# Up projections of a four-layer trunk: one matmul over 512 latent columns in place of two over 256

## The chip, the cores and the metric

The kernel runs on one core of a Trainium2 chip. The metric is device microseconds of one execution, as the median of three runs. The profile is one further execution, recorded by the hardware profiler; times in it are microseconds from the start of its span, unless marked ns.

## What is computed

A trunk of four layers over 512 latent tokens and 256 context tokens with 1024 channels, in fp32. Each layer normalises, modulates by vectors made from a conditioning vector, mixes tokens (short gated convolution in layers 0 and 3, windowed attention in layer 1, differential attention in layer 2), and then runs a ConvGLU with 2816 inner channels. Cut to what matters:

```python
def conv_ffn(x, w_up, conv_w, conv_b, w_down):
    a, g = jnp.split(x @ w_up, 2, axis=-1)
    g = dwconv(g, conv_w) + conv_b
    return (jax.nn.silu(g) * a) @ w_down

def short_conv_mixer(x, w_in, w_conv, w_out):
    b_gate, c_gate, h = jnp.split(x @ w_in, 3, axis=-1)
    return (b_gate * dwconv(c_gate * h, w_conv)) @ w_out

for i in range(DEPTH):
    xn = modulate(rmsnorm(h, g1), sh1, sc1)
    ...
    h = h + gt1 * y
    h = h + gt2 * conv_ffn(modulate(rmsnorm(h, g2), sh2, sc2), *ffns[i])
    if ctx_after:
        hc = hc + cg1 * yc
        hc = hc + cg2 * conv_ffn(modulate(rmsnorm(hc, g2), ch2, cc2), *ffns[i])
```

The context stream takes part up to the mixer of layer 2; from layer 2's ConvGLU on there are latents alone.

## The kernel before

Activations lie with channels on the 128 partitions and tokens along the columns: 8 chunks of channels, `hL` with 512 latent columns and `hC` with 256 context columns each. The streams are cut into parts of 256 columns: `CTXS` (the context), `H0` and `H1` (the halves of the latents); `LAT` stands for all 512. `parts_of` turns regions (`CTXS`, `LAT`) into parts.

**Precision.** Every operand of a large product is kept as two numbers, a rounded one and the rest (`wh` and `wl` of a weight, `xh` and `xl` of an activation), and `mm3` (L160 to L162) issues three matmuls for each product: `wh` by `xh`, `wh` by `xl`, `wl` by `xh`. The first operand is the stationary one, 128x128, and each matmul has a weight load of its own (engine PEld).

**Phases.** There are eight: a mixer and a ConvGLU in each layer. At the end of one, `boundary` weaves the last down products, part by part, with the norm of the next phase (`norm_steps`): squares, statistics, then for each chunk a modulated value (`nt`, L376), its rounded part by ScalarE (`xh`, L377) and the rest by VectorE (`xl`, L382). Each part has tiles of its own for `xh` and `xl`, 256 columns wide, 8 chunks each. They lie in a pool that is opened anew for each phase on the side `self.xside`, with the other tiles of a mixer or ConvGLU (`gp`, `cv`, `mh`, `ml`) on the opposite side. The side is left at first (L1127), and each attention mixer turns it over when it ends (L875 for layer 1, L1102 for layer 2).

**Up projections.** `project` computes one output chunk of 128 channels: for each part, 8 chunks of input channels by three matmuls into a PSUM tile `ps` (two of them, 1024 columns each: latents in columns 0 to 511, context behind them), or into `pb` for some. The first few projections of a phase are begun by `phase_start` for all parts but the last and finished later, when the last part's norm is there; they are named `pre` in the trace, both pieces of them. The others go through `projected` at once and carry the names `pg` and `pa` (ConvGLU) and `pc`, `ph`, `pb` (convolution). `phase_start` takes two projections where both streams run and four where the latents run alone.

**Units.** A ConvGLU has 22 units: `pg` is copied to `gp` (L575), the convolution's taps run on VectorE (L508 to L510), silu on ScalarE, and the product with `pa` is split into `mh` and `ml`. A convolution mixer has 8, of `pc`, `ph` and `pb`. Units go up two at a time and come down through `down_steps`: products `pd`, latents over 512 columns in one matmul, context over 256, added to `hL` and `hC` by VectorE (L430). The attention mixers project tokens instead (`tok_project`, L670 to L672, name `pj`): there the x tile, 128 tokens of it, is the stationary operand and 512 columns of weights move.

**Side work.** The modulation vectors of later phases are computed in between by VectorE (L289) and summed over partitions by GpSimd (`partition_all_reduce`, L291), once for each stream that needs the vector (`ada_vecs`, L237).

**Order.** Every engine's instructions are put in order when the kernel is built, by a scheduler that places waits where tiles are written and read; only a few DMAs and splits are pinned to the order of the program.

Of the kernel before, what the change touches and what calls it, by code (L numbers as in the profile page):

```python
# [10 lines left out]
F32R = mybir.dt.float32r  # L11
# [34 lines left out]
class Trunk:  # L46
# [1 line left out]
        self.tc, self.nc, self.A, self.out, self.stop = tc, tc.nc, A, out, stop  # L48
        self.xside = "left"

    # ---------------------------------------------------------------- weights
    def plan_weights(self):
        A = self.A
        w = []
# [55 lines left out]
        return hi, lo  # L110

    def prefetch(self, n):
        """Splits the next n weights, one a step, and lifts the limit."""
        for _ in range(n):
            if len(self.wready) < self.wpos + 5:
                self._split(True)
            self.wlimit = max(self.wlimit, len(self.wready))
            yield
# [10 lines left out]
        self.wready[i] = None  # L129
        return r  # L130

    # ---------------------------------------------------------------- helpers
    def ps(self, name):
        return self.pp.tile([P, 1024], F32, name=name, tag="ps", bufs=2)

# [40 lines left out]
            self.nc.tensor.matmul(ps[:, t * P:(t + 1) * P], r[:, t:t + 1].to_broadcast([P, P]), self.ident,  # L176
                                  start=True, stop=True)

    # ---------------------------------------------------------------- setup
    def setup(self, es):  # L180
        tc, nc, A = self.tc, self.nc, self.A
        self.cp = cp = es.enter_context(tc.tile_pool(name="const", bufs=1))
# [49 lines left out]
        for k in range(KC):  # L232
            self.tc.keep_in_program_order(self.nc.sync.dma_start(self.h[0][k], self.A["x"][k]))

    # ---------------------------------------------------------------- ada
    def ada_vecs(self, l, m):
        return (0, 1) if l < 2 or (l == 2 and m < 2) else (0,)  # L237

    def ada_first(self):
        """Shift and scale of the first norms: a chunk of channels at a time, straight on the tensor engine."""  # L240
        nc = self.nc
        for j in range(KC):
            if j in EARLY:
                self._fetch(True)
                self._split()
            acc = self.pb(f"adaf{j}")
            for i in range(2):
                raw = self.first.tile([P, KC // 2, 2 * P], F32, name=f"adaf{j}_{i}", tag="raw", bufs=5)
                self.tc.keep_in_program_order(nc.sync.dma_start(raw, self.A["l0_ada_first"][j, i]))
                for k in range(KC // 2):  # L250
                    nc.tensor.matmul(acc[:, :2 * P], self.cwide[:, i * KC // 2 + k], raw[:, k],
                                     start=i + k == 0, stop=i * k == KC // 2 - 1)
            row = self.ntmp("adarow")[:, :2 * P]
            nc.scalar.copy(row, acc[:, :2 * P])
            for m in range(2):
                nc.tensor.transpose(acc[:, (2 + m) * P:(3 + m) * P], row[:, m * P:(m + 1) * P], self.ident)
            cols = acc[:, 2 * P:].rearrange("p (m v e) -> p m v e", m=2, v=2)[:, :, :, 0]
            md = self.cp.tile([P, 2, 2], F32, name=f"md{j}", tag="md", bufs=KC)
            nc.vector.tensor_tensor(md, cols, self.ada_b[0][:, 0:2, j:j + 1].to_broadcast([P, 2, 2]), ALU.add)
            gs = self.cp.tile([P, 2], F32, name=f"gs{j}", tag="gs", bufs=KC)  # L260
            nc.vector.scalar_tensor_tensor(gs, md[:, 1, :], 1.0, self.g1[0][:, j:j + 1].to_broadcast([P, 2]),
                                           ALU.add, ALU.mult)
            self.mods1.append((md[:, 0, :], gs))
            yield
# [41 lines left out]
            if next(self.ada, "end") == "end":  # L306
                break

    # ---------------------------------------------------------------- norm
    def norm_steps(self, l, s, second, first):  # L310
        """RMS norm and modulation of one stream: a step for the square of each chunk, then the rest.
        The first norms scale the chunks by the statistics before the modulation is there."""
        nc = self.nc
        sid, T, off = s
        xp = self.xp
# [37 lines left out]
        yield  # L353
        rb = pst[:, T:2 * T]
        self.bcast_cols(rb, r, nt)
        xs, ts = [], []
        self.xn_next[s] = xs
        for k in range(KC):
            hi = xp.tile([P, T], F32R, name=f"xh{sid}_{off}_{k}", tag=f"xh{sid}", bufs=KC * (2 - sid))
            lo = xp.tile([P, T], F32R, name=f"xl{sid}_{off}_{k}", tag=f"xl{sid}", bufs=KC * (2 - sid))  # L360
            xs.append((hi, lo))
            if first:
                t = self.first.tile([P, T], F32, name=f"nt{sid}_{off}_{k}", tag="nt", bufs=3 * KC)
                nc.vector.tensor_tensor(t, h[k], rb, ALU.mult)
                ts.append(t)
# [17 lines left out]
            if k % 2 or first:  # L383
                yield

    # ---------------------------------------------------------------- pair structure
    def project(self, src, xn, parts, name, acc=None, split=False):
        """Projects some parts of the streams; acc is what an earlier call for other parts returned."""
        if acc is None:
            if split:  # L390
                out = {sid: self.pb(name) for sid, _, _ in parts}
            else:
                ps = self.ps(name)
                out = {0: ps[:, :SEQ], 1: ps[:, SEQ:TOK], "all": ps}
            acc = self.get_w(src), out
        (wh, wl), out = acc
        for s in parts:
            sid, T, off = s
            o = out[sid][:, off:off + T]
            for k in range(KC):  # L400
                xh, xl = xn[s][k]
                w = slice(k * P, (k + 1) * P)
                self.mm3(o, wh[:, w], wl[:, w], xh, xl, k == 0, k == KC - 1)
        return acc

    def phase_start(self, srcs, xn, regions):
        """The first projections of a phase leave the last part of the streams to the end."""
        n = PRM["nb"] if len(regions) == 2 else PRM["nl"]
        self.pre = [self.project(src, xn, parts_of(regions)[:-1], f"pre{i}", split=i >= 2) for i, src in enumerate(srcs[:n])]

    def projected(self, src, xn, regions, name):
        parts = parts_of(regions)
        if self.pre:
            return self.project(src, xn, parts[-1:], name, self.pre.pop(0))[1]
        return self.project(src, xn, parts, name)[1]

    def down_steps(self, units, ws, gate, parts, pools):
        nc = self.nc
# [12 lines left out]
                    yield  # L431

    def begin(self, s, first=False):
        """The norm of stream s for the phase that follows, if it takes part there."""
        if self.next is None or s not in parts_of(self.next[1]):
            return iter(())
        if self.xn_next is None:
            self.close_x()
            self.open_x()
            self.xn_next = {}  # L440
        return self.norm_steps(self.next[0], s, self.next[2], first)

    def boundary(self, seq, gate, before=()):
        """The last down products, stream by stream, woven with the norms of the next phase."""
        prev = list(before)
        for s, units, ws, last in seq:
            nrm = self.begin(s) if last else iter(())
            for _ in self.down_steps(units, ws, gate, [[s]], (self.pt, self.pb)):
                next(nrm, None)
                for g in prev:  # L450
                    next(g, None)
            if last:
                for g in prev:
                    for _ in g:
                        pass
                prev = []
            prev.append(nrm)
        for g in prev:
            for _ in g:
                pass  # L460

    def timeline(self, tasks, rate):
        """Interleaves generators: each task (begin, end, steps, generator) takes its steps evenly over its slots,
        and the filler takes rate steps a slot."""
        live = []
        tasks = sorted(tasks, key=lambda t: t[0])
        at, due, end = 0, 0.0, max(t[1] for t in tasks)
# [61 lines left out]

    @staticmethod  # L530
    def pair_order(n):
        """Units go up and down in groups, each going down while the next goes up; the last four go down together."""
        order = []
        for g in range(0, n - 2, GRP):
            order += [("up", c) for c in range(g, g + GRP)]
            if g:
                order += [("down", c) for c in range(g - GRP, g)]
        return order + [("up", n - 2), ("up", n - 1)] + [("down", c) for c in range(n - 4, n)]
# [66 lines left out]
        gate = {sid: self.mods[l, sid][:, 2, :] for sid, _, _ in streams}  # L605
        self.pairs(KC, up, A[f"l{l}_sc_out"], gate, streams, ticks)

    # ---------------------------------------------------------------- attention pieces
    def rope_table(self, l, which, yt):
        """Gain, and cosine and sine with the gain in them, of one of q and k."""  # L610
        nc, A = self.nc, self.A
        g = yt.tile([P, 2, HD], F32, name=f"gain{l}{which}")
        nc.sync.dma_start(g, A[f"l{l}_gain"][:, "qk".index(which)])
# [58 lines left out]
                mm(o, xh, wl[:, w], start=False, stop=k == KC - 1)  # L672
            post(tt, o)

    # ---------------------------------------------------------------- layer 1 mixer
    def window_gqa(self, xn):
        nc, A = self.nc, self.A
        yc = self.tc.tile_pool(name="y1", bufs=1, side=self.yside)
# [203 lines left out]
        self.boundary([(H1, final[H1], ws[1], True)], gate, [nrm, nrm0])  # L882
        mc.__exit__(None, None, None)

    # ---------------------------------------------------------------- layer 2 mixer
    def diff_attn(self, xn):
        nc, A = self.nc, self.A
        yc = self.tc.tile_pool(name="y2", bufs=1, side=self.yside)
# [214 lines left out]
        self.boundary([(s, *self.last, True) for s in (H0, H1)], gate)  # L1103
        mc.__exit__(None, None, None)

    # ---------------------------------------------------------------- whole
    def run(self):
        tc, nc = self.tc, self.nc
        es = ExitStack()
# [183 lines left out]
```

## Time and profile before

| what | value |
|---|---|
| median of the runs | 3337.18 us |
| runs | 3334.94, 3337.18, 3341.43 us |
| span of the profiled execution | 3339.3 us |
| what the profile shows around the span | nothing |
| mean granted TensorE clock | 0.972 of 2.4 GHz |
| matmuls | 22364 |

The profiled execution has no time of its own beside its span; the span lies 2.1 us above the median of the runs and within their range. Engines are PE (TensorE's matmuls), PEld (its weight loads), DVE (VectorE), ACT (ScalarE), POOL (GpSimd) and SP (SyncE). Matmuls overlap in the pipeline, and their ends are modelled, so their durations add up to more than the time that they take.

### The profile page before, as it was taken

The numbers are of one execution on the slowest core, as the hardware profiler recorded it, in microseconds if no ns is written. First come the engines' busy times: TensorE is split into PE (matmuls) and PEld (weight loads), VectorE is DVE, ScalarE is ACT, GpSimd is POOL, SyncE is SP. The second block draws the span as 40 slices with busy tenths as digits, with TensorE's granted clock in tenths as the row PEclk, the third lists the DMA queues.
The fourth block names the chain that finished last, engine by engine and source line by source line (L and its number), as shares of the span: only waits on it lengthen the run. The fifth ranks groups of instructions, "written<-read, shape, count | busy, mean of one in ns | idle before, by whom it ended". The sixth has DMA issues, their size and how long they took to land.

```text
span 3339.3 us, 53917 instructions
## 1 busy us (share of the span) xinstructions
PE 3272.2 (98%) x22364; PEld 2979.7 (89%) x22364; DVE 2207.4 (66%) x3278; ACT 1127.0 (34%) x1888; POOL 686.3 (21%) x578
## 2 busy tenths in 40 slices
PE   8999999999998999999999999999999999999999
PEld 7999999989986778999999987677899999999999
DVE  5775887786565676676666576366687765565555
ACT  4113322222333565422222243356432323242222
POOL 2132223211132333111000134255211110010000
PEclk9999999999996899899999999899999999999999
DMA  6431443442110000333333112401265532222322
GB/s 226 139 108 52 152 132 110 134 132 77 52 65 19 14 21 6 102 108 113 110 127 112 60 54 79 142 29 54 68 202 161 179 112 89 95 89 84 101 89 76
DMA packets 105237, 323.29 MB, mean 97 GB/s; under 512 B 12576, under 2 KB 27552, under 8 KB 104992
## 3 DMA queue, kind: packets, MB, share of 16 engines
q1 hardware_dynamic: 100512, 313.26, 29.0%
q0 software_dynamic: 4480, 6.58, 0.9%
q8 instruction: 176, 2.88, 0.3%
q14 instruction: 69, 0.57, 0.1%
HBM read 311.26 MB, written 8.53 MB: 96 GB/s over the span
## 4 chain that ended last, share of the span: by engine, by line
PE 93%; DVE 4%; ACT 1%; DMA 1%; issue 1%; POOL 0%; SPq 0%; ACTq 0%; DVEq 0%; POOLq 0%
PE pd L160 8%; PE pd L161 8%; PE pd L162 8%; PE pa L161 6%; PE pa L160 6%; PE pa L162 6%; PE pg L160 6%; PE pg L162 6%; PE pg L161 6%; PE pj L670 3%; PE pj L671 3%; PE pj L672 3%; PE psS L980 2%; PE pO L826 2%; PE pPT L816 1%; PE psS L979 1%
## 5 line engine op out<-in xcount | busy, mean ns | idle before, releaser
L108 ACT CAST wh<-wr 128x1024 fp32r<-128x1024 f32 x380 | 392.2, 1049 | 1282.1 <-issue 524.9
L109 DVE TENSOR_TENSOR wl<-wr,wh 128x1024 fp32r<-128x1024 f32 x380 | 497.9, 1323 | 233.0 <-ACT wh L108 231.6
L160 PE MATMUL pd<-mh,wh 128*128 128x256 f32 (+1 forms) x1712 | 568.6, 333 | 9.9 <-DVE hC L430 9.2
L161 PE MATMUL pd<-ml,wh 128*128 128x256 f32 (+1 forms) x1712 | 564.1, 330 | 0.3 <-DVE ml L1057 0.3
L162 PE MATMUL pd<-mh,wl 128*128 128x256 f32 (+1 forms) x1712 | 563.7, 329 | 0.0
L430 DVE SCALAR_TENSOR_TENSOR hL<-pd,mod,hL 128x512 f32<-128x512 f32 (+1 forms) x512 | 335.6, 660 | 249.7 <-PE pd L162 248.2
L160 PE MATMUL pg<-xh,wh 128*128 128x256 f32 x1648 | 465.5, 282 | 1.5 <-ACT gp L575 1.5
L162 PE MATMUL pg<-xh,wl 128*128 128x256 f32 x1648 | 465.3, 282 | 0.0
L162 PE MATMUL pa<-xh,wl 128*128 128x256 f32 x1648 | 465.3, 282 | 0.0
L160 PE MATMUL pa<-xh,wh 128*128 128x256 f32 x1648 | 465.3, 282 | 0.0
L161 PE MATMUL pa<-xl,wh 128*128 128x256 f32 x1648 | 465.3, 282 | 0.0
L161 PE MATMUL pg<-xl,wh 128*128 128x256 f32 x1648 | 465.2, 282 | 0.0
L291 POOL PARTITION_ALL_REDUCE acc<-acc x34 | 222.9, 6587 | 1130.8 <-DVE acc L289 1130.8
L160 PEld LDWEIGHTS pd<-mh,wh 128*128 128x128 f32 x1712 | 325.8, 190 | 39.0 <-DVE hC L430 9.6
L162 PEld LDWEIGHTS pd<-mh,wl 128*128 128x128 f32 x1712 | 326.4, 191 | 30.8
L161 PEld LDWEIGHTS pd<-ml,wh 128*128 128x128 f32 x1712 | 326.4, 191 | 25.6 <-DVE ml L1057 0.5
L289 DVE SCALAR_TENSOR_TENSOR acc<-adaw,csilu,acc 128x1024 f32<-128x1024 f32 x238 | 297.8, 1279 | 47.5 <-DMA adaw<-l_ada_w 44.5
L160 PEld LDWEIGHTS pg<-xh,wh 128*128 128x128 f32 x1648 | 314.1, 191 | 5.5 <-ACT gp L575 1.7
L161 PEld LDWEIGHTS pg<-xl,wh 128*128 128x128 f32 x1648 | 314.0, 191 | 4.3
L162 PEld LDWEIGHTS pg<-xh,wl 128*128 128x128 f32 x1648 | 314.2, 191 | 2.1
L160 PEld LDWEIGHTS pa<-xh,wh 128*128 128x128 f32 x1648 | 314.6, 191 | 0.1
L161 PEld LDWEIGHTS pa<-xl,wh 128*128 128x128 f32 x1648 | 314.6, 191 | 0.1
(234 smaller groups left out, 6311.9 us busy)
## 6 DMA issues: line engine op xcount, KB each, us to landing
adaw<-l_ada_w SPq DMA_DIRECT2D x176, 512.0 KB, 3.7
wr<-l_ffn_up SPq DMA_DIRECT2D x176, 512.0 KB, 3.6
wr<-l_ffn_down SPq DMA_DIRECT2D x88, 512.0 KB, 3.6
wr<-l_sc_in SPq DMA_DIRECT2D x48, 512.0 KB, 3.6
wr<-l_da_qkv SPq DMA_DIRECT2D x24, 512.0 KB, 3.9
adaf<-l_ada_first SPq DMA_DIRECT2D x16, 512.0 KB, 5.7
wr<-l_sc_out SPq DMA_DIRECT2D x16, 512.0 KB, 3.6
wr<-l_wa_qkv SPq DMA_DIRECT2D x12, 512.0 KB, 3.8
```

Source lines behind the costliest of these rows:

```text
L108: keep(self.nc.scalar.copy(hi, raw))
L109: keep(self.nc.vector.tensor_tensor(lo, raw, hi.bitcast(F32), ALU.subtract))
L160: mm(ps, wh, xh, start=first, stop=False)
L161: mm(ps, wh, xl, start=False, stop=False)
L162: mm(ps, wl, xh, start=False, stop=last)
L289: keep(nc.vector.scalar_tensor_tensor(acc[v], raw, c, acc[v], ALU.mult, ALU.add))
L291: nc.gpsimd.partition_all_reduce(acc[v], acc[v], P, bass.bass_isa.ReduceOp.add)
L430: nc.vector.scalar_tensor_tensor(hk, ps, gate[sid][:, oc:oc + 1], hk, ALU.mult, ALU.add)
L670: mm(o, xh, wh[:, w], start=k == 0, stop=False)
L671: mm(o, xl, wh[:, w], start=False, stop=False)
L672: mm(o, xh, wl[:, w], start=False, stop=k == KC - 1)
L826: nc.tensor.matmul(po, vw, t, start=n == 1 and i == 0, stop=n == len(keys) and i == 1)
```

## The change

The norm gets one set of tiles for all 512 latent columns (`LAT`), made when the first half comes to it, and each half writes its own columns of them. Parts are slices of these tiles, so whoever asks for `H0` or `H1` finds them as before; `LAT` is there beside them. `projected` passes regions and not parts to `project`, so that the latents are one region of 512 columns there; `phase_start` and the finishing of what it began still go by parts. Besides, comments and docstrings are emptied, which changes no instruction; lines behind L356 move by two.

```diff
@@ norm_steps
         rb = pst[:, T:2 * T]
         self.bcast_cols(rb, r, nt)
-        xs, ts = [], []
+        whole = CTXS if sid else LAT
+        if whole not in self.xn_next:
+            self.xn_next[whole] = [[xp.tile([P, whole[1]], F32R, name=f"x{x}{sid}_{k}", tag=f"x{x}{sid}", bufs=KC)
+                                    for x in "hl"] for k in range(KC)]
+        xs = [[x[:, off:off + T] for x in xx] for xx in self.xn_next[whole]]
         self.xn_next[s] = xs
+        ts = []
         for k in range(KC):
-            hi = xp.tile([P, T], F32R, name=f"xh{sid}_{off}_{k}", tag=f"xh{sid}", bufs=KC * (2 - sid))
-            lo = xp.tile([P, T], F32R, name=f"xl{sid}_{off}_{k}", tag=f"xl{sid}", bufs=KC * (2 - sid))
-            xs.append((hi, lo))
             if first:
@@ projected
         parts = parts_of(regions)
         if self.pre:
             return self.project(src, xn, parts[-1:], name, self.pre.pop(0))[1]
-        return self.project(src, xn, parts, name)[1]
+        return self.project(src, xn, regions, name)[1]
```

## Rows read from the trace of the kernel before

**Rows 1.** The page: span, and busy time of each engine.
```profile
span 3339.3 us, 53917 instructions
PE 3272.2 (98%) x22364; PEld 2979.7 (89%) x22364; DVE 2207.4 (66%) x3278; ACT 1127.0 (34%) x1888; POOL 686.3 (21%) x578
```

**Rows 2.** The page: shares of the chain that ended last.
```profile
PE 93%; DVE 4%; ACT 1%; DMA 1%; issue 1%; POOL 0%; SPq 0%; ACTq 0%; DVEq 0%; POOLq 0%
```

**Rows 3.** Stretches of the ConvGLUs: length, busy PE PEld DVE ACT POOL, clock, DMA.
```profile
400.00:800.00 400.00, 395.55 (x2922) 377.72 (x2921) 318.75 (x366) 95.02 (x117) 107.27 (x42) 0.99 0.39 122
1400.00:1800.00 400.00, 395.19 (x2990) 379.16 (x2989) 265.70 (x314) 94.65 (x118) 55.18 (x21) 0.99 0.37 115
2400.00:2600.00 200.00, 199.89 (x1442) 188.88 (x1441) 158.34 (x174) 64.60 (x81) 31.08 (x12) 1.00 0.56 180
3000.00:3300.00 300.00, 300.00 (x2097) 280.50 (x2096) 172.89 (x213) 82.46 (x106) 0.00 (x0) 1.00 0.29 92
```

**Rows 4.** Groups of TensorE's instructions by form: busy, mean ns, idle before.
```profile
L160 PE MATMUL pg<-xh,wh 128*128 128x256 f32 x1648 | 465.5, 282 | 1.5 <-ACT gp L575 1.5
L160 PE MATMUL pa<-xh,wh 128*128 128x256 f32 x1648 | 465.3, 282 | 0.0
...
L160 PE MATMUL pd<-mh,wh 128*128 128x512 f32 x688 | 274.4, 399 | 0.2
...
L670 PE MATMUL pj<-wh,xh 128*128 128x512 f32 x400 | 158.9, 398 | 5.4 <-DVE pt L638 5.3
...
L160 PE MATMUL pb<-xh,wh 128*128 128x256 f32 x304 | 86.0, 283 | 0.0
...
L160 PE MATMUL ph<-xh,wh 128*128 128x256 f32 x280 | 79.2, 283 | 0.0
...
L160 PE MATMUL pc<-xh,wh 128*128 128x256 f32 x264 | 74.6, 283 | 0.0
```

**Rows 5.** Stretches, `pa` alone: length, busy PE PEld DVE, clock, DMA.
```profile
361.20:370.20 9.00, 8.80 (x72) 8.66 (x72) 0.00 (x0) 1.00 0.68 222
1466.30:1475.30 9.00, 8.68 (x72) 8.51 (x72) 0.17 (x1) 1.00 0.41 131
2465.10:2471.30 6.20, 5.92 (x48) 5.74 (x48) 0.00 (x0) 1.00 0.80 264
```

**Rows 6.** Stretches, `pj` alone: length, busy PE PEld DVE ACT, clock, DMA.
```profile
967.55:1015.50 47.95, 47.86 (x210) 39.34 (x210) 6.21 (x9) 4.79 (x9) 1.00 0.11 33
1985.20:1993.45 8.25, 8.17 (x34) 6.28 (x34) 1.38 (x2) 1.20 (x2) 1.00 0.00 1
```

**Rows 7.** A stretch of layer 2's ConvGLU, `pd` alone.
```profile
2470.85:2476.80 5.95, 5.76 (x24) 4.36 (x24) 2.24 (x3) 1.00 0.56 175
```

**Rows 8.** Waits of PE: us in total, times, longest.
```profile
PE pd L160 <- DVE hC L430: 9.2, 2, 4.8
...
PE pre L161 <- DVE xl L382: 4.3, 7, 1.0
```

**Rows 9.** Timeline around 713 us (start, us), and L509's durations (ns, min/median/max).
```profile
706.06 13.45 POOL L291 PARTITION_ALL_REDUCE acc<-acc  x2 [39.44 <-DVE acc L289]
...
713.59 5.17 DVE L509 SCALAR_TENSOR_TENSOR cv<-gp,pack,cv 128x769 f32<-128x769 f32 x1
...
722.19 0.58 PE L160 MATMUL pd<-mh,wh 128*128 128x256 f32 x1 [4.41 <-DVE hC L430]
...
L509 DVE SCALAR_TENSOR_TENSOR cv<-gp,pack,cv x104: 740/1012/5169, 72.0 to 3309.8; 128x769 f32<-128x769 f32 x52, 128x512 f32<-128x512 f32 x52
```

**Rows 10.** Start of layer 3's mixer: `pre` alone in a stretch; the last `xl`.
```profile
2765.00:2785.90 20.90, 15.63 (x121) 14.82 (x122) 0.00 (x0) 0.00 (x0) 1.00 0.32 102
...
2785.88 0.48 DVE L382 SCALAR_TENSOR_TENSOR xl<-nt,mod,xh 128x256 fp32r<-128x256 f32 x1 [0.18 <-ACT xh L377]
```

## The prediction

> **What bounds the kernel now.** I read the page's busy shares first [rows 1]: TensorE is busy 98% of a span of 3339.3 us and VectorE 66%. Because matmuls overlap in the pipeline, such a share alone could hide idle time, so next came the chain that ended last [rows 2]: 93% of it is TensorE, 4% VectorE. The stretches agree [rows 3]: in the ConvGLU of layers 0, 1, 2 and 3 TensorE's row covers 98.8 to 100% of the time at a granted clock of 0.99 to 1.00, while VectorE is at 80%, 66%, 79% and 58%. What counts there is therefore how far apart matmuls start. The duration in the rows of lines (282 ns for 256 columns, 399 ns for 512) is no price, since the next matmul starts long before an earlier one ends [rows 4].
>
> The step from start to start comes from unbroken runs: a run's busy time less the duration of its last matmul, divided by the number of steps. 72 `pa` matmuls of 256 columns in layer 0 take 8.80 us: (8.80 - 0.28)/71 = 120.0 ns. In layer 2, 48 take 5.92 us: 120.0 ns. In layer 1, 72 take 8.68 us: 118.3 ns [rows 5]. For 512 columns the kernel has two kinds of run. In the qkv projection of layer 1, 210 `pj` matmuls take 47.86 us: (47.86 - 0.40)/209 = 227.1 ns. In that of layer 2, 34 take 8.17 us: (8.17 - 0.40)/33 = 235.5 ns [rows 6]. The down projections' `pd` are between: 24 take 5.76 us, (5.76 - 0.40)/23 = 233.0 ns [rows 7]. So one matmul over 512 columns costs less than two over 256, by 1 to 13 ns, and the whole case is that difference and how often it is had.
>
> **How often.** Each `project` over one part issues 8 chunks x 3 products = 24 matmuls, 8 from each of L160 to L162. `pg` and `pa` show 1648 a line, that is 206 parts each [rows 4]: 21 units x 3 parts in layers 0 and 1 (126) and 20 x 2 in layers 2 and 3 (80). The missing units are those that `phase_start` begins; they run under the name `pre` and keep their parts, as the diff leaves `parts[:-1]` and `parts[-1:]` alone. So 82 `pg` and 82 `pa` projections each merge two latent halves. By the same division `pc` (33 parts) merges 7 + 6, `ph` (35) 7 + 7, `pb` (38) 8 + 7. Together 82 + 82 + 13 + 14 + 15 = 206 projections x 24 = 4944 pairs, which become 4944 matmuls; as many weight loads go. What `pre` began, the context part and all `pd` stay as they are.
>
> **The price of a pair.** No run shows an up projection of 512 columns, so its step is bounded by the nearest rows: 227.1 ns below, 235.5 ns above. Which holds where? The code puts the pool of x tiles on the left side until layer 1's mixer ends (L1127), on the right for layer 1's ConvGLU and layer 2's mixer (L875), and on the left again afterwards (L1102). The rows sort themselves by that: with x on the left the 256 step is 120.0 and the qkv step 227.1; with x on the right they are 118.3 and 235.5 [rows 5, 6]. These `pj` runs read the same x tiles, only as the stationary operand, so they are the nearest rows; `pd` reads other tiles. I take 227.1 for the left and 235.5 for the right. That the place of the tiles is the cause is an inference from four runs.
>
> Left: layer 0 (22 conv and 42 ConvGLU projections), layer 2 (40), layer 3 (20 and 40) are 164 x 24 = 3936 pairs at 240.0 - 227.1 = 12.9 ns, 50.8 us. Right: layer 1, 42 x 24 = 1008 pairs at 236.6 - 235.5 = 1.1 ns, 1.1 us. Sum 51.9 us. With `pd`'s 233.0 on the right it would be 54.4; with 235.5 on both sides 17.7 + 1.1 = 18.8; with 227.1 on both 50.8 + 9.6 = 60.4.
>
> A rule speaks against this size. The rows put the part of the step that does not grow with columns at 2 x 120.0 - 227.1 = 12.9 ns on the left. The Trainium skill, "TensorE: Matmul & The Clock Gate", section "Wait — 56ns, not 53.3ns?", has a warm step of columns over 2.4 GHz plus about 2.5 ns, so that a pair would save 2.5 ns and 4944 pairs 12.4 us, an estimate by that page. By that rule 256 columns would take 109 ns and 512 take 216; this trace has 118 to 120 and 227 to 236, so it does not agree on the fixed part.
>
> **What else the edit touches, at nothing.** The bytes of the x tiles are the same (32 tiles of 256 columns become 16 of 512), and the norm still writes each half by its own instructions, so ScalarE and VectorE keep theirs. A merged matmul needs both halves at once: every merged projection stands behind the rest of `pre`, which has read the second half already, and `pre` holds both `ps` buffers until then; TensorE runs these in that order. If that cover were gone, the cost is the third rival below. No DMA is added or moved. VectorE must keep up with a faster TensorE: layer 2's stretch of 200 us holds some 12 units (a unit is 48 x 0.120 + 48 x 0.120 + 24 x 0.233 = 17.1 us), each shorter by 48 x 12.9 ns = 0.62 us, so VectorE's 158.3 us fall into 192.7, 82% instead of 79% [rows 3]. PSUM's evacuation stays ahead on average; queued behind a slow VectorE instruction are the L430 updates that free `pd`.
>
> The profile's span stands 2.1 us above the runs' median of 3337.18, and nothing beyond the span is shown, so the 51.9 us come off the median: **3285 us**, 1.6% faster.
>
> **Rivals.** *512 columns at the slow step on the left too.* For it: `pd` runs at 233.0 in the same stretches [rows 7], and the left/right sorting rests on few runs. Against it: the run at 227.1 is the longest of all, 210 matmuls [rows 6]. At 233.0 a left pair saves 7.0 ns: 27.6 + 1.1 = 28.7 us, 3308; at 235.5, 18.8 us, 3318.
>
> *Hardly any fixed part.* All pairs save what layer 1's do, 236.6 less 233.0 to 235.5, or 1.1 to 3.6 ns: 5 to 18 us, 3319 to 3332. The page's rule would end here. The even 120.0 on the left speaks against it.
>
> *VectorE gives it back.* Beside a pair of `partition_all_reduce` (13.45 us) one L509 took 5.17 us where its median is 1.01, and TensorE then waited 4.41 us [rows 9]. Only two such waits occur, 9.2 us together [rows 8]. Where a modulation vector is computed for both streams the code issues such a pair (L237, L290), 12 times in all, so ten pass without a wait now; the less slack a faster TensorE leaves VectorE, the more of them will show. At 4.6 us each, three more give 3299, ten more 3331; without today's two, 3276.
>
> *Slower: readers of the first half wait for the writer of the second.* Both now write one tile. If the wait is for the tile, `pre` on the first half can't start until the second half's norm is done. In the last phase but one, 121 `pre` matmuls overlap the time before the last `xl` is written [rows 10]; as the norm's chunks come one after another, I put the exposed part at half of that, 60 x 0.12 = 7 to 8 us, at 8 phase starts 56 to 64 us, less 51.9: 3341 to 3349 when counted from the median, and more if the clock falls in the gap. It decides once over 52 us in all are exposed. No row shows which it is; today's starts show little waiting (L161 4.3 us in all, [rows 8]). The halves are disjoint columns, so a wait by place and not by tile would see no conflict.
>
> That the change doesn't do what it says can be left out: 512-column forms of the same three lines run today [rows 4].
>
> **How the numbers follow.** Forecast 0.60, own range 3264 (both waits gone, the right side at 227.1, 3 us of the runs' spread) to 3298 (two more waits, the same spread); slow step on the left 0.20; hardly any fixed part 0.06; VectorE 0.10; slower 0.04. Up to 3316 the range takes in most of the slow step and part of the VectorE case, leaving out under 2 in 10. A measurement of this kernel tells about 0.2%, 6.7 us (three runs spread over 6.5). Within that fall the top ends of the second and third cases, 0.03; slower 0.04; faster 0.93.
>
> **What would show it.** Right: `pa` L160 splits into 336 of 256 and 656 of 512 columns, TensorE's matmuls fall by 4944 from 22364 (a few records can be missing), and runs of 512 step at 227 on the left, 233 to 236 in layer 1; the ConvGLU stretches stay at 99 to 100%. Wrong: a left step of 233 or more; waits of `pd` on L430 well over 9.2 us; `pre` waiting for `xl` for tens of us.

## The result, and the profile after

The changed kernel takes 3276.68 us (median of four runs, 3271.39 to 3282.38) against 3336.06 us for the kernel before in the same runs: a ratio of 0.983, 95% interval 0.9809 to 0.9852. It is 1.7% faster, 59.4 us by the medians and 58.7 us by the spans of the two profiled executions, 3339.3 [rows 1] and 3280.6. The forecast was 3285 us, a gain of 51.9 us.

The page: span, busy times, and the shares of the chain that ended last.

```profile
span 3280.6 us, 43984 instructions
...
PE 3214.6 (98%) x17420; PEld 2721.1 (83%) x17420; DVE 2202.1 (67%) x3278; ACT 1126.6 (34%) x1888; POOL 684.6 (21%) x578
...
PE 93%; DVE 4%; ACT 1%; DMA 1%; issue 1%; POOL 1%; SPq 0%; ACTq 0%; POOLq 0%; DVEq 0%
```

TensorE has 4944 matmuls and as many weight loads fewer than in [rows 1], exactly the forecast count, and its share of the span and of the chain stands where it was [rows 1, 2]. The other engines' busy times and counts have hardly moved.

Stretches inside the ConvGLUs of layers 0, 1, 2 and 3, with the columns of [rows 3]; they begin a little earlier than there, since everything ahead of them is shorter.

```profile
395.00:790.00 395.00, 389.96 (x2225) 343.04 (x2224) 319.45 (x370) 97.54 (x120) 102.65 (x41) 0.99 0.37 123
1385.00:1780.00 395.00, 390.11 (x2204) 339.50 (x2203) 263.45 (x312) 92.72 (x116) 55.17 (x21) 0.99 0.34 116
2375.00:2575.00 200.00, 200.00 (x913) 165.47 (x912) 164.06 (x182) 68.94 (x86) 31.08 (x12) 1.00 0.58 192
2950.00:3250.00 300.00, 300.00 (x1310) 245.52 (x1309) 174.64 (x217) 87.06 (x110) 0.00 (x0) 1.00 0.27 92
```

TensorE still fills 98.7 to 100% of each at the same granted clock, so the distance between matmuls still sets the time. VectorE in layer 2 is at 164.06 of 200 us, 82%, the share that the prediction worked out.

TensorE's groups by form, as in [rows 4].

```profile
L160 PE MATMUL pg<-xh,wh 128*128 128x512 f32 x656 | 257.1, 392 | 0.0
L160 PE MATMUL pa<-xh,wh 128*128 128x512 f32 x656 | 256.5, 391 | 0.0
...
L160 PE MATMUL pa<-xh,wh 128*128 128x256 f32 x336 | 94.6, 281 | 0.0
L160 PE MATMUL pb<-xh,wh 128*128 128x512 f32 x120 | 46.8, 390 | 0.0
L160 PE MATMUL ph<-xh,wh 128*128 128x512 f32 x112 | 43.7, 390 | 0.0
L160 PE MATMUL pc<-xh,wh 128*128 128x512 f32 x104 | 40.6, 391 | 0.0
```

The merged forms make 656 + 656 + 120 + 112 + 104 = 1648 a line, 206 projections of 8, and three lines of them are the 4944.

Next, unbroken runs of 24 `pa` of 512 columns, with the columns of [rows 5]: in layer 1 (its x26 takes in two matmuls of 256 that are ending when the stretch begins), then in layer 2; and 22 `pd` of 512 in layer 2, as in [rows 7].

```profile
1449.85:1455.70 5.85, 5.76 (x26) 4.33 (x24) 0.00 (x0) 1.00 0.32 106
2389.90:2395.70 5.80, 5.60 (x24) 4.33 (x24) 0.00 (x0) 1.00 0.83 291
...
2439.72:2445.15 5.43, 5.30 (x22) 3.96 (x22) 2.15 (x3) 1.00 0.61 206
```

Less the last matmul's duration of 0.39 to 0.40 us, the steps are 5.37/23 = 233.5 ns in layer 1, 5.21/23 = 226.5 ns in layer 2, and 4.90/21 = 233.3 ns for `pd`. The left side is at the forecast's 227; layer 1 is at the low end of its 233 to 236.

TensorE's waits, as in [rows 8].

```profile
PE pd L160 <- DVE hC L432: 9.9, 2, 5.0
...
PE pre L161 <- DVE xl L384: 4.0, 6, 1.0
...
PE pre L160 <- ACT xh L379: 3.0, 4, 1.1
```

The waits behind the slow VectorE instruction are still two, 9.9 instead of 9.2 us, and `pre` waits 4.0 us for `xl` instead of 4.3.

**Where the 58.7 us are.** I cut both traces at the first matmul of each phase. The phases with x tiles on the left shrink by 8.7 (layer 0's mixer), 11.3 (layer 0's ConvGLU), 12.0 (layer 2's), 6.1 and 11.6 (layer 3's mixer and ConvGLU): 49.7 us. Layer 1's ConvGLU gives 4.5. The ConvGLUs and layer 3's mixer repeat within 0.5 us from one profile to another (the change and its repetition in experiment 7; the kernel before and experiment 1, which merges nothing). Layer 0's mixer repeats less well: without merging it has 270.6 and 268.5 us, so some 2 of its 8.7 us may not be the edit's. What is left, 4.6 us, lies where no pair is merged: layer 2's mixer is 6.3 us shorter, layer 1's and the start of the kernel 1.7 longer. The first 45 us of layer 2's attention show how; the first row is of the kernel before, the second of the kernel after, from the same place in the work (columns as in [rows 3]).

```profile
2134.50:2180.00 45.50, 40.58 (x111) 24.23 (x110) 18.56 (x30) 20.63 (x46) 20.20 (x23) 0.55 0.28 91
```
```profile
2111.80:2157.00 45.20, 41.94 (x126) 24.75 (x124) 21.10 (x34) 23.48 (x52) 21.09 (x25) 0.62 0.27 90
```

The granted clock is 0.62 where it was 0.55, so 126 matmuls fit where 111 did. Both are mixtures of the two levels, 1.2 and 2.4 GHz, in a stretch where TensorE has gaps. Such a difference needn't be the edit's: the first experiment shows one of 10.5 us in layer 1's mixer with no merged matmul at all. For layer 2's mixer it stays open. It took 447.5 and 447.8 us in the two kernels that merge nothing, about 441 in five executions with merged pairs (the change, its repetition, experiments 2, 4 and 5), and 448.8 in another one with them (the second kernel of experiment 3).

### The profile page after: what moved, and what is told of

Read it like the earlier page. It is cut to its first block, busy times and chain, and to the rows that moved or that the text cites. A ratio compares the mean times of both kernels' runs of the same rounds, so it can differ in the third digit from the quotient of the medians.

```text
span 3280.6 us, 43984 instructions
## 1 busy us (share of the span) xinstructions
PE 3214.6 (98%) x17420; PEld 2721.1 (83%) x17420; DVE 2202.1 (67%) x3278; ACT 1126.6 (34%) x1888; POOL 684.6 (21%) x578
## 4 chain that ended last, share of the span: by engine, by line
PE 93%; DVE 4%; ACT 1%; DMA 1%; issue 1%; POOL 1%; SPq 0%; ACTq 0%; POOLq 0%; DVEq 0%
PE pd L160 9%; PE pd L161 8%; PE pd L162 8%; PE pg L160 6%; PE pg L162 6%; PE pg L161 6%; PE pa L161 6%; PE pa L162 6%; PE pa L160 6%; PE pj L672 3%; PE pj L673 3%; PE pj L674 3%; PE psS L982 2%; PE pO L828 2%; PE pPT L818 1%; PE psS L981 1%
## 5 line engine op out<-in xcount | busy, mean ns | idle before, releaser
L160 PE MATMUL pg<-xh,wh 128*128 128x256 f32 (+1 forms) x992 | 352.4, 355 | 1.5 <-ACT gp L577 1.5
L161 PE MATMUL pg<-xl,wh 128*128 128x256 f32 (+1 forms) x992 | 352.1, 355 | 0.0
L162 PE MATMUL pg<-xh,wl 128*128 128x256 f32 (+1 forms) x992 | 352.1, 355 | 0.0
L161 PE MATMUL pa<-xl,wh 128*128 128x256 f32 (+1 forms) x992 | 351.2, 354 | 0.0
L160 PE MATMUL pa<-xh,wh 128*128 128x256 f32 (+1 forms) x992 | 351.1, 354 | 0.0
L162 PE MATMUL pa<-xh,wl 128*128 128x256 f32 (+1 forms) x992 | 351.0, 354 | 0.0
L289 DVE SCALAR_TENSOR_TENSOR acc<-adaw,csilu,acc 128x1024 f32<-128x1024 f32 x238 | 300.9, 1293 | 59.4 <-DMA adaw<-l_ada_w 58.8
L160 PEld LDWEIGHTS pg<-xh,wh 128*128 128x128 f32 x992 | 187.6, 189 | 28.5 <-ACT gp L577 1.7
L162 PEld LDWEIGHTS pg<-xh,wl 128*128 128x128 f32 x992 | 187.6, 189 | 27.3
L160 PEld LDWEIGHTS pa<-xh,wh 128*128 128x128 f32 x992 | 187.0, 188 | 27.0
L162 PEld LDWEIGHTS pa<-xh,wl 128*128 128x128 f32 x992 | 186.9, 188 | 27.0
```

The source lines that it names most:

```text
L160: mm(ps, wh, xh, start=first, stop=False)
L161: mm(ps, wh, xl, start=False, stop=False)
L162: mm(ps, wl, xh, start=False, stop=last)
L289: keep(nc.vector.scalar_tensor_tensor(acc[v], raw, c, acc[v], ALU.mult, ALU.add))
```

## The experiments

None of the kernels leaves out or changes part of the computation. Medians are given with their extremes, and ratios against runs of the kernel before on the same chip (3337.8, 3335.47 and 3335.23 us in the three groups).

**1. The shared tile without the merged matmul.** Tiles of 512 columns as in the change, but two matmuls of 256 over their halves.

```diff
-        return self.project(src, xn, regions, name)[1]
+        return self.project(src, xn, parts, name)[1]
```

> One set of x tiles for 512 latent columns as in the change, but the up projections in two matmuls over halves, as before. Theory (each matmul carries a part of its step that does not grow with columns, so that only the merging saves): the steps are 120.0 ns on the left and 118.3 in layer 1, matmuls are 22364 again, and the time is that of the kernel before, 3323 to 3341 us. Rival (the shared tiles or the order that follows from them brought the gain): the time stays near 3277. Slower rival of the prediction (a wait for the tile and not for its half): starts of phases wait for xl for tens of us, over 3380.

Measured: 3332.95 us (3324.71 to 3339.92), ratio 0.9997 (0.9981 to 1.0013). The count of matmuls and the step are those of before: 72 `pa` in layer 0, with the columns of [rows 5],

```profile
359.50:368.60 9.10, 8.80 (x72) 8.60 (x72) 0.00 (x0) 1.00 0.69 224
```

that is 120.0 ns. By phases its ConvGLUs and layer 3's mixer are within 0.2 us of those before. So the wider tile alone costs nothing and gains nothing, and the gain of the edited phases is the merge. Its profiled span, 3327.2 us, is 12.1 us under that of before, and 10.5 of these are layer 1's mixer (419.9 instead of 430.4 us), which has no edit. The first 100 us of its attention, in this kernel, then in the one before, which comes there 2 us later (columns as in [rows 3]):

```profile
1000.00:1100.00 100.00, 87.08 (x321) 59.63 (x321) 60.38 (x136) 47.85 (x111) 33.94 (x39) 0.74 0.09 27
```
```profile
1002.00:1102.00 100.00, 89.07 (x300) 61.61 (x299) 53.18 (x120) 41.92 (x95) 30.60 (x34) 0.64 0.08 27
```

A granted clock of 0.74 instead of 0.64, and 21 matmuls more in less busy time. Runs of one and the same kernel spread by such amounts (the kernel before: 3324.55 us at a mean clock of 0.977, 3341.26 at 0.971), which is why steps and phase lengths are compared here as well as medians.

**2. The x tiles moved by 32 bytes where they lie on the left.** The prediction priced the step by the side of the tiles. This separates the side, and the layer, from the address: in the programs as built, the tiles of x on the left and those of the weights start 256 bytes past a multiple of 512, and the x tiles on the right 480 past one. (The addresses come from the build and stand in no trace; that the moves below shift them by so many bytes follows from the edits.)

```diff
             self.open_x()
+            if self.xside == "left":
+                pad = self.xp.tile([P, 8], F32, name="xpad")
+                self.nc.gpsimd.memset(pad, 0.0)
```

> The changed kernel with every pool of x tiles on the left moved by 32 bytes. Theory (where the moving tile begins sets the step of 512 columns): on the left the pg, pa, pb, ph and pc steps go from 227 to 233 ns, layer 1 stays at 233, and 3936 matmuls lose 6 ns each, 24 us: about 3300. Rival (layer 1 has the slower step for its own work: its VectorE load, its transfers, or the weights that it reads): the left stays at 227 and the time at 3277.

Measured: 3292.87 us (3287.75 to 3299.3), ratio 0.9881 (0.9856 to 0.9907). Runs of 24 `pa` in layers 1 and 2, 24 `pa` of 256 columns in layer 0 up to the start of the next matmul, then the 210 `pj` in layer 1 that [rows 6] show at 227.1 ns:

```profile
1442.05:1447.90 5.85, 5.76 (x26) 4.33 (x24) 0.00 (x0) 1.00 0.40 116
2381.92:2387.85 5.93, 5.76 (x24) 4.33 (x24) 0.00 (x0) 1.00 0.89 310
...
353.33:356.13 2.80, 2.80 (x24) 2.79 (x24) 0.00 (x0) 1.00 0.41 126
...
950.70:1000.20 49.50, 49.23 (x210) 39.39 (x210) 6.21 (x9) 4.88 (x9) 1.00 0.10 32
```

Layer 2's step is now layer 1's, (5.76 - 0.395)/23 = 233.3 ns, and `pj` steps at (49.23 - 0.40)/209 = 233.6. Neither the side nor the layer makes the slow step; the place of the x tile does, also where x is the stationary operand, as in `pj`. By phases the left gives back 15.0 us, less than 3936 x 6 ns = 24 us. Some 5 us of the difference are the steps of 256 columns, which fell from the 120.0 ns of [rows 5] to 2.80/24 = 116.7 in layer 0 (1536 of them on the context).

**3. The tiles on the right moved by 32, 96 and 224 bytes.** If the place does it, layer 1 can be had at 227 too. A small pool is put at the right edge; N is 8, 24 and 56 (448, 384 and 256 bytes past a multiple of 512).

```diff
         self.WR, self.WS = 3, 5
+        rp = es.enter_context(tc.tile_pool(name="rpad", bufs=1, side="right"))
+        nc.gpsimd.memset(rp.tile([P, N], F32, name="rpad"), 0.0)
```

With 32 bytes:

> The changed kernel with everything on the right side moved by 32 bytes: the x tiles of layer 1's ConvGLU and of layer 2's mixer, and the mh and ml tiles that the down projections of layers 0, 2 and 3 move. Theory (place of the tiles): layer 1's pg and pa go from 233 to 227 ns (1008 matmuls, 6 us), layer 2's pj from 234 to 227 (768, 5 us), and pd over 512 columns in layers 0, 2 and 3 from 233 to 227 (some 1400, 8 us), while pd over 256 columns goes from 118.4 to 120.0 there (about 2000, 3 us back): about 16 us faster, 3261. Rival (work of the layer): no step moves, 3277.

With 32 bytes, and the `cv` buffer made 56 bytes longer, which moves the tiles of `pd`:

> As the one before, and the buffers of the taps are made 56 bytes longer, so that mh and ml of layer 1's ConvGLU, on the left, begin at multiples of 64 bytes too. Theory: layer 1's pd over 512 columns joins at 227 ns (some 500 matmuls, 3 us less, with 1 us back on 256 columns): 3258 to 3262. Rival: 3277, as the changed kernel.

With 96 bytes:

> The changed kernel with everything on the right side moved by 96 bytes and not by 32. In the programs as built the x tiles of layer 1 then begin at a multiple of 128 bytes, as those on the left do; moved by 32 bytes they began 64 bytes past one, and unmoved 96 past one. Theory (a multiple of 128 bytes gives the 227 ns): layer 1's pg and pa over 512 columns go to 227 ns (1008 matmuls, 6 us), layer 2's pj to 227 (768, 5 us), pd over 512 columns of layers 0, 2 and 3 to 227 (some 1400, 8 us), with 2 to 4 us back on 256 columns: 3260 to 3264. Rival (in layer 1 and in pd the slower step comes from the layer's other work, VectorE's load above all, and the place only ever made the left worse): 233 stays for both, 3269 as with 32 bytes.

With 96 bytes and both `gp` and `cv` buffers of 3200 bytes:

> As the one before, and the buffers of gates and taps made 3200 bytes long, so that every mh and ml tile begins at a multiple of 128 bytes, those of layer 1's ConvGLU too. Theory: all pd over 512 columns at 227 ns (2064 matmuls, 12 us), x as before: 3255 to 3261. Rival: pd stays at 233, 3269.

Measured: 3268.66 us (3267.22 to 3277.67; ratio 0.9808, 0.9787 to 0.983), 3269.87 (3268.85 to 3284.33; 0.9819, 0.9796 to 0.9842), 3270.43 (3269.46 to 3270.88; 0.9812, 0.9786 to 0.9837) and 3270.23 (3269.83 to 3270.72; 0.9811, 0.9786 to 0.9837). The steps missed what was expected. In layer 1, a run of 24 `pa` of 256 columns and the 24 of 512 behind it with 32 bytes, and 24 of 512 with 96 bytes:

```profile
1364.42:1367.15 2.73, 2.72 (x24) 2.72 (x24) 0.00 (x0) 1.00 0.54 170
1367.15:1372.95 5.80, 5.76 (x26) 4.33 (x24) 0.00 (x0) 1.00 0.56 193
...
1364.53:1370.30 5.77, 5.75 (x26) 4.35 (x24) 0.00 (x0) 1.00 0.51 180
```

The step stays at (5.76 - 0.40)/23 = 233.0 ns with 32 bytes and is (5.75 - 0.39)/23 = 233.0 with 96. So neither a multiple of 32 nor one of 128 is enough. The few us gained come from elsewhere. With 32 bytes layer 1's 256-column step fell from 118.3 [rows 5] to 2.72/24 = 113.3 ns, which the idea didn't foresee and which stays unexplained. And layer 2's `pj`, 34 in this row, went more than half of the way:

```profile
1950.60:1958.70 8.10, 8.03 (x34) 6.31 (x34) 1.38 (x2) 1.20 (x2) 1.00 0.00 0
```

Their first step is 0.30 us long, as before; the other 32 take (8.03 - 0.39 - 0.30)/32 = 229.4 ns instead of 233.1 (worked out below, under layer 1). With 96 bytes, 10 of the 12 us by which the profiled span is shorter than the changed kernel's lie in layer 1's mixer, whose length varies by as much without an edit (experiment 1).

With 224 bytes, so that x starts at a multiple of 256, as on the left:

> The changed kernel with everything on the right side moved by 224 bytes. In the programs as built the weights' tiles begin 256 bytes past a multiple of 512, as the x tiles on the left do; on the right they began 480 past one unmoved, 448 with 32 bytes and 384 with 96, and all three were slow. With 224 they begin 256 past one. Theory (the 227 ns need the moving tile at a multiple of 256 bytes): layer 1's pg and pa go to 227 ns (6 us), layer 2's pj to 227 (5 us), pd over 512 columns in layers 0, 2 and 3 to 227 (8 us), 2 to 4 us back on 256 columns: 3255 to 3263. Rival (the right side itself is slower, wherever the tile begins): 232 to 233 ns stay, 3268 to 3277.

Measured: 3257.33 us (3255.02 to 3271.01), ratio 0.9778 (0.9756 to 0.98). Runs of 24 `pa` in layers 1 and 2, of 22 `pd` in layer 2, and of 34 `pj` in layer 2:

```profile
1437.50:1443.25 5.75, 5.63 (x26) 4.33 (x24) 0.01 (x1) 1.00 0.41 118
2369.88:2375.60 5.72, 5.60 (x24) 4.34 (x24) 0.00 (x0) 1.00 0.85 302
...
2419.30:2424.55 5.25, 5.15 (x22) 3.96 (x22) 2.15 (x3) 1.00 0.57 183
...
1976.40:1984.50 8.10, 7.95 (x34) 6.30 (x34) 0.68 (x1) 0.60 (x1) 1.00 0.39 127
```

Layer 1's step falls from 233.5 to (5.63 - 0.39)/23 = 227.8 ns, `pd` in layer 2 from 233.3 to 4.75/21 = 226.2, and layer 2's `pj` from the 235.5 of [rows 6] to 7.55/33 = 228.8; both of the last take in a first step of 0.30 us, and without it they are 233.1 and (7.55 - 0.30)/32 = 226.6. All three were slow and all three moved with the address alone.

By phases, against experiment 7, the places that moved give 17.2 us: 5.4 in layer 1's ConvGLU, 4.5 in layer 2's mixer, 7.2 in layers 2 and 3 behind it, 0.1 in layer 0. The other 10 of the 27.4 us between the two spans are the start and layer 1's mixer (9.3), whose length varies by as much without an edit (experiment 1).

With 224 bytes and a `cv` buffer of 784 floats, which moves `pd`'s tiles in layer 1 as well:

> As the one before, with the buffers of the taps 56 bytes longer, so that mh and ml of layer 1's ConvGLU, on the left, begin at a multiple of 512 bytes, that is 256 bytes off from the weights modulo 512. Theory: layer 1's pd over 512 columns goes from 233 to 227 ns as well, some 500 matmuls, 3 us: 3252 to 3261. If 256 bytes are not enough and 512 from the weights are needed, this pd stays at 233 while all others go to 227. Rival (the right side itself): no step moves but perhaps this one, 3268 to 3277.

Measured: 3256.44 us (3255.21 to 3269.52), ratio 0.9775 (0.9754 to 0.9797): the fastest median, 2.2% under the kernel before and 0.8% under the changed kernel run again beside it. The last edit alone is worth nothing that can be told: `pd` of 512 in layer 1 steps at 230.3 ns as a mean, between the two levels. The mean is a mixture. These runs are six matmuls long; the first row is of six behind matmuls of 256 columns, the second of six behind 512:

```profile
1465.08:1466.70 1.62, 1.55 (x6) 0.95 (x6) 1.08 (x3) 1.00 0.01 3
1474.63:1476.30 1.67, 1.52 (x6) 0.94 (x5) 0.10 (x1) 1.00 0.00 0
```

That is (1.55 - 0.39)/5 = 232 ns and (1.52 - 0.39)/5 = 226 ns. Behind 256 columns the five steps are 233, 236, 229, 232 and 231 ns long, and the runs of 24 `pa` in layer 0 of the changed kernel open with the same five before they settle at 227. So this `pd` has the fast level too, and with the addresses of its expectation, 256 bytes off the weights modulo 512, a multiple of 256 is enough.

**4. The left moved by 128 bytes.** A control for the last two, from the other side: if a multiple of 256 is what counts, the left must lose with 128 as it did with 32 (N = 32 in the edit of experiment 2).

> The changed kernel with the x tiles on the left moved by 128 bytes. Theory of 256 bytes: the left's steps over 512 columns go from 227 to about 232.5 ns, what the right had at a multiple of 128 bytes only: 3936 x 5 ns, 20 us, 3293 to 3299. Rival (the right side itself, and on the left only tiles off a multiple of 128 bytes are slow): 227 ns stay, 3277.

Measured: 3297.8 us (3292.49 to 3298.8), ratio 0.9887 (0.9871 to 0.9904). A run of 24 `pa` in layer 2:

```profile
2439.38:2445.15 5.77, 5.74 (x24) 4.33 (x23) 0.00 (x0) 1.00 0.78 258
```

The left's step is (5.74 - 0.39)/23 = 232.6 ns. As expected.

**5. The latents cut at 384 instead of 256.** The same columns and the same count of matmuls as before, in other widths, to price the part of a step that doesn't grow with columns.

```diff
-            o = out[sid][:, off:off + T]
-            for k in range(KC):
...
+            cuts = ((0, 384), (384, 512)) if T == SEQ else ((0, T),)
+            for a, b in cuts:
+                o = out[sid][:, off + a:off + b]
...
+                    self.mm3(o, wh[:, w], wl[:, w], xh[:, a:b], xl[:, a:b], k == 0, k == KC - 1)
```

> The changed kernel, but where it moves 512 latent columns at once it moves 384 and then 128, all 24 of the one and then all 24 of the other. Theory that each matmul has a fixed part of 13 ns and the rest is 0.417 ns a column: 173 ns and 67 ns, 240 for a pair, the kernel's time near that of before, 3325 to 3340 us. Rival that what is fixed is the weight load, which must fit behind the matmul ahead of it and which a long matmul hides: 384 columns still take 173 ns, but 128 columns take what the transposes of 128 columns take today, 109 ns or more, so a pair takes 282 or more and the kernel some 270 us longer than the changed one, 3550 us or more.

Measured: 3552.93 us, one run. A run of `pa` in layer 2: 24 of 384 columns up to the start of the next, then 24 of 128.

```profile
2533.93:2538.16 4.23, 4.23 (x25) 4.23 (x26) 0.00 (x0) 1.00 0.68 211
2538.16:2541.20 3.04, 2.79 (x25) 2.64 (x24) 0.00 (x0) 1.00 0.84 303
```

The wide step is 4.23/24 = 176.3 ns and the narrow one (2.79 - 0.27)/23 = 109.6 ns, as means that take in the switch from one width to the other. Together 285.9 ns, against means of 227.6 on the left and 233.0 in layer 1: 3936 x 58.3 + 1008 x 52.9 = 283 us, and the run is 276 us above the changed kernel. Without the first two matmuls of each width, where a step of 229 and one of 60 ns stand:

```profile
2534.69:2538.15 3.46, 3.46 (x21) 3.46 (x21) 0.00 (x0) 1.00 0.84 258
2538.33:2541.20 2.87, 2.62 (x24) 2.47 (x23) 0.00 (x0) 1.00 0.82 301
```

Twenty wide steps take 3.46 us, 173 ns each, and 21 narrow ones 2.62 - 0.27 us, 112 ns each. From 256 columns to 512 a step grows by 226.5 - 120.0 = 106.5 ns, 0.416 ns a column, which is one cycle at 2.4 GHz. At that rate 256, 384 and 512 columns last 106.7, 160.0 and 213.3 ns; the steps stand about 13 ns above that at all three widths (120.0 in [rows 5], 173, and 226.5), while 128 columns, 53.3 ns, take 59 more. Below some width between 128 and 256 the columns no longer set the step of these matmuls. What does is not shown. The weight load is one reading: one goes with every matmul, and in the narrow run PEld is busy 2.47 of the 2.62 us. But a load of 128 columns has no fixed price, as a row of the kernel before shows:

```profile
1993.22 0.81 PE L165 MATMUL pkt<-identr,ks 128*128 128x128 f32 x8
```

These eight transposes of 128 columns, each with a load of its own, start (0.81 - 0.25)/7 = 80 ns apart; those of `pPT` start 109 ns apart (the median in the trace at a full clock). The Trainium skill, "TensorE: Matmul & The Clock Gate", section "LDWEIGHTS (loading the stationary operand)", has a load of 128 columns take columns over 1.2, an estimate of 107 ns; the narrow step and `pPT` lie 2 to 5 ns above it, `pkt` 27 below.

**6. No head start.** Nothing is begun on the first half, so that every phase waits for both halves' norms. That is what the slower rival supposed the shared tile to force.

```diff
-            if f == 0:
+            self.pre = []
+            if False:
                 self.phase_start
```

(and the same at the mixer's start.)

> The changed kernel without the early start of a phase: no projection of the ConvGLUs and convolution mixers begins before the norm of the second latent half is done, and all are over 512 columns. This prices the prediction's slower rival, in which a reader of the first half waits for the writer of the second. Its estimate was 7 to 8 us a start: at the 6 starts that this edit touches 42 to 48 us, less 5 us for 432 more merged pairs, so 3314 to 3320. Rival (the early start hides little): 3272 to 3285.

Measured: 3318.14 us (3307.21 to 3318.94), ratio 0.9946 (0.9931 to 0.9961). Its count of matmuls is 16988: 432 more pairs merge, worth 432 x 12.9 ns = 5.6 us, and yet its profiled span is 36.0 us longer than the changed kernel's. So 41.6 us are exposed at six phase starts, 6.9 us each as a mean, near the 7 to 8 of the prediction. By phases they are far from alike: the span grows by 4.5 us in all at the three starts where the context runs too and its part of a projection comes first, and by 16.9, 6.2 and 9.1 at the three with latents alone, layer 2's ConvGLU and both phases of layer 3. (The 16.9 stand in layer 2's mixer, which varies by some 6 us.) TensorE's waits show the places:

```profile
PE nps L176 <- POOL rstd L171: 8.8, 5, 2.8
PE pg L160 <- ACT xh L379: 7.4, 5, 3.1
PE nps L348 <- ACT nsl L335: 7.3, 5, 2.0
```

And the clock adds to them. The start of layer 3's mixer, first in this kernel, then in the changed one (columns as in [rows 3]):

```profile
2745.00:2775.00 30.00, 22.90 (x97) 18.76 (x96) 21.33 (x41) 12.98 (x23) 1.48 (x8) 0.83 0.32 106
```
```profile
2705.00:2735.00 30.00, 29.91 (x253) 29.69 (x252) 21.21 (x45) 12.91 (x28) 8.55 (x18) 1.00 0.14 47
```

With the head start TensorE has no gap and keeps the clock at 1.00. Without it the stretch has gaps, 7.1 us of it, and a granted clock of 0.83. Over the whole span TensorE idles 3316.6 - 3231.9 = 84.7 us instead of 66.0; the other 22.9 of the 41.6 us are, by subtraction, matmuls that take longer. The mean granted clock, 0.965 instead of 0.973, fits that.

**7. The changed kernel again,** on the same chip as x moved by 224 bytes and experiment 4.

> The changed kernel once more, beside the others on the same chip: 3271 to 3282 as in the comparison of the change. Were it nearer 3268, the moves of 32 and 96 bytes brought nothing.

Measured: 3282.17 us (3271.57 to 3295.84), ratio 0.984 (0.9814 to 0.9866). The result repeats.

## Why the prediction was right, point by point

**The bound.** Right. TensorE's starts set the time in the edited phases before and after, and the gain is there: 54.2 of 58.7 us. Experiment 1 leaves no part of these to the tiles.

**How often.** Right to the pair: 4944.

**The left, 50.8 us.** Right: 49.7 by phases, and the trace's 3936 steps on the left have a mean of 227.6 ns. That the sum is so close is in part luck: the four phases that repeat well give 41.0 us where the forecast has 44.0 (in layer 0 the first steps behind 256 columns are longer, experiment 3), and layer 0's mixer gives 8.7 for 6.8, some 2 us of which may be its own variation. The row to trust was the run of 210 `pj`, which reads x tiles at the same place; `pd`, at 233 in the same stretches, would have given 27.6, and it was slow because of its own tiles' address (experiment 3).

**Layer 1, 1.1 us.** Mis-sized: 4.5 by the phase. The term that failed is the new step of 235.5 ns, from 34 `pj` of layer 2 [rows 6]. That run isn't even; its first two matmuls in the kernel before are

```profile
1985.22 0.47 PE L672 MATMUL pj<-wl,xh 128*128 128x512 f32 x1
1985.53 0.39 PE L670 MATMUL pj<-wh,xh 128*128 128x512 f32 x1
```

0.31 us apart, and the other 32 steps are (8.17 - 0.40 - 0.31)/32 = 233.1 ns. Layer 1's new step is 233.0 to 233.5. A pair so saves 3.1 to 3.6 ns and 1008 pairs 3.1 to 3.6 us. The remaining 1 us I have no row for. In the run of 210 the same first step weighs less than half a nanosecond, which is why 227.1 held and 235.5 didn't.

**The sorting by sides.** The prediction called it an inference from four runs. As a sorting it held; as a cause it fell. The steps of 512 in even runs were 226 to 228 ns with x at a multiple of 256 bytes, 232.6 to 233.6 where it stood 32, 128, 192 or 224 bytes past one, on either side; the one exception is `pj` at 192 past, 229.4. What stays open: whether a multiple of 256 counts or the same place as the weights' modulo 256, since the weights were never moved; why this `pj` is between the levels; why the first steps behind 256 columns are longer; and why some shifts shorten the steps of 256.

**The remaining gain.** The forecast lies 7 us short by spans: 3.4 of layer 1, less 1.1 of the left, and 4.6 in the mixers of layers 1 and 2, with a higher granted clock in layer 2's, that no step of the prediction was about.

**The rivals.** *The slow step on the left* didn't happen, but experiment 2 built it, with 32 bytes: 3293 us where the rival was priced at 3308. Some 5 us of that distance are the steps of 256 that fell too, and 2 are layer 1; the rest is not worked out. *Hardly any fixed part* fell with the left's step: 2 x 120.0 - 226.5 = 13.5 ns saved a pair. The rule that spoke against the size (the Trainium skill, "TensorE: Matmul & The Clock Gate", section "Wait — 56ns, not 53.3ns?", about 2.5 ns a matmul) doesn't hold for these matmuls, each with a weight load of its own: experiment 5 has about 13 ns at three widths. *VectorE gives it back* didn't occur: two waits before, two after, 0.7 us more. Those ten pairs of `partition_all_reduce` that showed no wait still show none. *Slower* didn't occur either: with one tile for both halves `pre` waits 4.0 and 3.0 us in all, so a reader of the first half doesn't wait for the writer of the second. Its price was right where it was taken, at layer 3's mixer: 6.2 us by phases, and 1.2 that merged pairs save in the phase before (experiment 6). That the mean, 6.9, is near it too is luck, as the starts differ from next to nothing to 17 us. And it counted eight starts where six begin with `pre`, so that the kernel would then have been at about 3318 + 5.6 = 3324 us, still faster than before.

## What to carry to other kernels

Where TensorE is the bound, price a matmul by the step of an unbroken run of the same width over the same tiles, and multiply by a count from the rows: here that gave the gain of the edited phases within 5% (51.9 of 54.2 us). Take the step from a long run, or leave its first matmul out: one long step in a run of 34 made 235.5 of 233.1 ns and a term three times too small. Look up where the operands' tiles start before taking a step from a neighbour: with 224 bytes of padding on one side the median fell by another 25 us (3282.17 to 3257.33), some 17 of which lie in phases where steps fell. And before two pieces of work are made to share a tile or an instruction, see what was begun early on one of them: the head start on the first half is worth 41.6 us here, more than half of it, by subtraction, through the clock.

## What the runs showed of the hardware that was not expected

- The step of a 512-column matmul depends on the start address of its operands in the partition: 226 to 228 ns in even runs with all of them at multiples of 256 bytes, 232.6 to 233.6 with one of them 32, 128 or 224 bytes off, whether it is the moving or the stationary one. At 192 bytes off it was 233.0 for the moving operand and 229.4 for the stationary one.
- For 256 columns the same shifts act the other way or not at all: 120.0 ns on the left unmoved, 116.7 with 32 bytes; 118.3 in layer 1 unmoved, 113.3 with 32 bytes.
- The first five steps of 512 columns behind matmuls of 256 are longer even with all operands at multiples of 256 bytes: 232 ns as a mean against 226 behind 512.
- An up product of 128 columns with its own weight load steps at 112 ns, only 8 ns less than one of 256, so halving the width from 256 gives next to nothing here; transposes of 128 columns stepped at 80 (`pkt`) and 109 ns (`pPT`).
